# A hybrid decoder trunk on eight cores: two programs chosen by a per-core role instead of one program with a flag

## The chip, the cores and the metric

One Trainium2 chip, eight cores, one launch. Each of four sequences of 4096 tokens is shared by two cores: the even one has the first part, the odd one the second. The metric is device time in microseconds (us) of the slowest core. Some executions fall into a slower state, in which the cores of a die (cores 0 to 3, or 4 to 7) show a lower granted clock (TensorE's clock, as a share of full speed); they are kept apart, and only fast runs (or the cores of the undisturbed die) are compared. TensorE does the matmuls (PE in the profiles; PEld are its weight loads), VectorE (DVE), ScalarE (ACT) and GpSimd (POOL) the rest; SyncE (SP) and GpSimd issue the transfers (DMA).

## The reference, cut to what matters

```python
D_MODEL, BATCH, SEQ = 2048, 4, 4096
def reference(x, ...):
    h = x
    # layer 0: mLSTM, 8 heads, causal convolution of 4 taps on q and k, a state
    #   (C: 256x512, n: 256 per head) carried from the first token to the last
    h = h + mlstm_layer(rmsnorm(h, g0), ...)
    # layer 1: gMLP, spatial gating inside chunks of 128 tokens
    h = h + gmlp_layer(rmsnorm(h, g1), ...)
    return rmsnorm(h, gf)
```

Only the mLSTM state and three tokens of the convolution tie the second part of a sequence to the first. A chunk below is 128 tokens; a sequence has 32.

## The kernel before

Every core runs the same program. A *prefix* of 16 chunks gets the state at the split cheaply: per pair of heads the weighted keys K, then G = X^T K, then C = G^T W_v, without values, outputs or layer 1. Then 16 main chunks run through both layers in tiles of 6, 5, 5 chunks; each tile reads all weights (72 tiles of 2048x512, float32 in memory, cast to bfloat16 by the transfer) once. On even cores the prefix computes the wrong thing, and its outcome is multiplied by a flag of 0.

```python
MAIN = [6, 5, 5]
PRE = 16
...
        sizes = {16: [1, 1, 2, 3, 3, 3, 3], 17: [1, 2, 2, 3, 3, 3, 3]}[P]   # token groups of the k projection
...
        def nb_(c):                      # norm of prefix chunk c; its result is spilled to memory
            norm_b(px[c % 3][:], [pxb[c % 3]], pn[c % 2][:], pnb[c % 2], sl[c])
            xld(c + 3)
            dma("sp", xwsem[c % 2], xs_d[:, :, c * 256:(c + 1) * 256]..., pn[c % 2][:]..., R=[pnb[c % 2]], W=[xsd_b[c]])
        def run_stage(i):
            if i < P: na(i)              # square and sum on ScalarE
            if 0 <= i - 1 < P: nb_(i - 1)
            if 0 <= i - 2 < P: nc_(i - 2)    # transposes on TensorE, copies on ScalarE
            ...
        def xload():                     # the spilled activations come back, 1 MB at a time, 32 times, two buffers
            ...
            dma("sp", xrsem[i], XSt[:, i, 0:P, :]..., xs_d[j][:, 0:P * 256], R=xsd_b, W=[XSb[i]])
        def gpair(hp, jp, k):            # one group of G = X^T K: P matmuls of 512 columns
            ...
        def cgrp(hp, hh, cc, wi, q):
            ...
            dve([pkb, flagb], [cstgb[cc]], "tensor_scalar", out=cstg[:, cc, :], in0=pk[:, :], scalar1=flag[:, 0:1], ...)
...
    prefix(PRE, 0)
    for t in range(len(MAIN)):
        layer0(t, False)
        ...
```

The softmax here doesn't subtract the row's maximum and nothing guards it: scores larger than these inputs give would overflow.

Of the kernel before, what the change touches and what calls it, by code (L numbers as in the profile page):

```python
# [14 lines left out]
D = 2048  # L15
KC = 16
H = 8
EPS = 1e-6
NMAX = 6
PMAX = 16  # L20
MAIN = [6, 5, 5]
PRE = 16
NTOK = sum(MAIN) * 128
NPRE = PRE * 128
XP = 4 + NMAX * 128
XPP = 4 + PMAX * 128

# [180 lines left out]
def build_program():  # L208
    nc = bass.Bass("TRN2", target_bir_lowering=False)
    dt = lambda n, s, k="ExternalInput", d=F32: nc.dram_tensor(n, s, d, kind=k).ap()  # L210
    xm_d = dt("xm", [NTOK, D])
    xp_d = dt("xp", [NPRE, D])
    flag_d = dt("flag", [128, 1])
    wt_d = dt("wt", [NTILE, 128, KC * 512])
    wg_d = dt("wg", [128, KC * 16])
    g0_d = dt("g0bc", [128, D])
    g1_d = dt("g1bc", [128, D])
    gf_d = dt("gfbc", [128, D])
    convw_d = dt("convw", [128, 32 * 4])
    convb_d = dt("convb", [128, 32])  # L220
    gateb_d = dt("gateb", [128, 16])
    hg_d = dt("hgbc", [128, 4096])
    lng_d = dt("lng", [128, 32])
    lnb_d = dt("lnb", [128, 32])
    wsT_d = dt("wsT", [128, 8 * 128])
    bs_d = dt("bsbc", [128, 8 * 128])
    maskT_d = dt("maskT", [128, 128])
    ident_d = dt("ident", [128, 128])
    out_d = dt("out", [NTOK, D], "ExternalOutput")
    cst_d = nc.dram_tensor("cst", [H, 128, 1024], F32).ap()  # L230
    rs_d = nc.dram_tensor("rsd", [128, 1024], F32).ap()
    xs_d = nc.dram_tensor("xsd", [8, 128, PMAX * 256], BF16).ap()

    with ExitStack() as es:
        sems = {k: es.enter_context(nc.semaphore("s_" + k)) for k in ("pe", "act", "dve", "pool", "sp")}
        dsems = [es.enter_context(nc.semaphore("d%d" % i)) for i in range(100)]
        mem = Mem(nc)
        PSN = ["PJ0", "PJ1", "PJ2", "PT", "PS", "PN", "PK0", "PK1"]
        banks = [es.enter_context(nc.psum_tensor("ps_" + n, [128, 512], F32)) for n in PSN]
        body(nc, mem, TK(nc, sems, dsems), banks, locals())  # L240
    return nc


def body(nc, mem, tk, banks, dr):
    xm_d, xp_d, wt_d, out_d = dr["xm_d"], dr["xp_d"], dr["wt_d"], dr["out_d"]
# [19 lines left out]
    G = const("G", [D], F32); Gb = G.buf()  # L265
    flag = const("flag", [1], F32); flagb = flag.buf()
    convw = const("convw", [32, 4], F32); convwb = convw.buf()
# [42 lines left out]
    XO = HO + NMAX * 8192  # L310
    assert XO + 24576 <= REND, (XO + 24576, REND)

# [8 lines left out]
    def gtemps(tag, o_, n):  # L321
# [8 lines left out]
    GTM, _e = gtemps("m", _e, NMAX)  # L330
    (xnb0, xnb1), _e = seq(XO + 16384, [("xnb0", [D], BF16), ("xnb1", [D], BF16)])
    STG = [[(t, t.buf()) for t in (xs0,)], [(t, t.buf()) for t in (xnb0, xnb1)]]
    HN = NMAX // 2 * 128
    (acc, qT, kT, kp, so, sz), _e = seq(XO, [
# [19 lines left out]
    ybfb = [ybf.buf(i, i * 1024, i * 1024 + 1024) for i in range(2)]  # L354
    (uT, szT, sv, bia, junk1), _e = seq(XO, [
        ("uT", [4, NMAX * 128], BF16), ("szT", [3, HN], BF16), ("sv", [2, HN], F32),
        ("bia", [2, 128], F32), ("junk1", [512], BF16)])
    uTb = [[uT.buf((d_, i)) for i in range(2)] for d_ in range(4)]
# [122 lines left out]
    def consts():  # L481
        dma("pool", tk.dsem(), ident[:], dr["ident_d"], W=[identb])
        wpiece()
        wpiece()
        dma("pool", tk.dsem(), wg[:].rearrange("p k c -> p (k c)"), dr["wg_d"], W=[wgb])
        wpiece()
        wpiece()
        cload(convw[:], dr["convw_d"].rearrange("p (c j) -> p c j", j=4), convwb)
        cload(convb[:], dr["convb_d"], convbb)
        cload(gateb[:], dr["gateb_d"], gatebb)  # L490
        cload(maskT[:], dr["maskT_d"], maskTb)
        cload(flag[:], dr["flag_d"], flagb)
        cload(lng[:], dr["lng_d"], lngb)
        cload(lnb[:], dr["lnb_d"], lnbb)
        for b_ in cbufs:
            b_.w = (cs.sem, cs.cnt, cs.key)
        for t_, b_, v_ in ((onesf, onesfb, 1.0), (onesb, onesbb, 1.0), (mhalf, mhalfb, -0.5)):
            tk.op("dve", lambda v, t_=t_, v_=v_: v.memset(t_[:], v_), (), [b_])
# [82 lines left out]
    def prefix(P, tile0):  # L581
        NP = P * 128
        sizes = {16: [1, 1, 2, 3, 3, 3, 3], 17: [1, 2, 2, 3, 3, 3, 3]}[P]
        tgs = [(128 * sum(sizes[:i]), 128 * sum(sizes[:i + 1])) for i in range(len(sizes))]
# [22 lines left out]
        cstgb = [cstg.buf(i, i * 2048, i * 2048 + 2048) for i in range(2)]  # L607
        PGT, _e = gtemps("p", A4 + 7168, P)
        assert _e <= REND, (_e, REND)
        px = [mem.at("px%d" % i, [D], F32, a) for i, a in enumerate((A1, A1 + 8192, A2))]  # L610
# [131 lines left out]
        def nsum(hp):  # L742
            mm(KPb + [onesbb], [PSb], [(PS[:, hh * 2 + cc:hh * 2 + cc + 1], KP[:, c, hh * 256 + cc * 128:hh * 256 + (cc + 1) * 128],
                                        onesb[:, 0:1], c == 0, c == P - 1) for hh in range(2) for cc in range(2) for c in range(P)])
            dve([PSb, flagb], nstb[hp * 2:hp * 2 + 2], "tensor_scalar", out=nst[:, hp * 2:hp * 2 + 2, :],
                in0=PS[:, 0:4].rearrange("p (h c) -> p h c", c=2), scalar1=flag[:, 0:1], scalar2=None, op0=ALU.mult)

        def cgrp(hp, hh, cc, wi, q):
# [5 lines left out]
            if q == 0:  # L754
                return
            dve([pkb, flagb], [cstgb[cc]], "tensor_scalar", out=cstg[:, cc, :], in0=pk[:, :], scalar1=flag[:, 0:1], scalar2=None, op0=ALU.mult)
            dma("sp", css[cc], cst_d[h][:, cc * 512:(cc + 1) * 512], cstg[:, cc, :], R=[cstgb[cc]], W=[])
# [50 lines left out]
        def save_halo():  # L808
            dve([XTb[P - 1], flagb], [halob], "tensor_scalar", out=halo[:, :, 1:4], in0=XT[:, :, 4 + NP - 3:4 + NP],
                scalar1=flag[:, 0:1], scalar2=None, op0=ALU.mult)  # L810
        S.at(S.last, save_halo)
# [57 lines left out]

    def layer0(t, zero_state):  # L870
        n = MAIN[t]
# [141 lines left out]
        def head_events(h, oid, vid, zid):  # L1013
            b = vid[0]
            S.at(oid[1], lambda: ktr(h, list(range(h0))))
            S.at(oid[2], lambda: cb0(h))
            S.at(oid[3], lambda: ktr(h, list(range(h0, n))))
            if h + 1 < H:
# [15 lines left out]
        for h in range(H):  # L1034
            qk(h)
            oid = tm(T_O, h, ev_o)
            vid = tm(T_V, h, ev_v)
# [165 lines left out]

    prefix(PRE, 0)
    for t in range(len(MAIN)):
        layer0(t, False)
        n = MAIN[t]
# [35 lines left out]
def _prep_inputs(inputs):  # L1243
# [38 lines left out]
    for c in range(8):  # L1282
        b, s = c // 2, c % 2
        m = dict(common)
        m["xm"] = np.ascontiguousarray(x[b, s * NTOK:(s + 1) * NTOK])
        m["xp"] = np.ascontiguousarray(x[b, 0:NPRE])
        m["flag"] = np.full((128, 1), float(s), np.float32)
        in_maps.append(m)
# [14 lines left out]
```

## Time and profile before

| | us |
|---|---|
| median of the first three runs | 4950.75 |
| profiled run, slowest core (3) | 4951.6 |
| of this: prefix, up to the first main q/k projection | 676.6 |
| tile of 6 chunks, tile of 5, last tile of 5 | 1599.3, 1336.9, 1338.9 |

How to read it: the tiles have TensorE busy nearly without a gap, so a tile costs its columns; the prefix has 98 us in which TensorE waits. All eight cores have a prefix: it ends between 662.1 us (core 1) and 676.6 us (core 3), and from there on every core takes the same 4275.0 us. So cores with the same work differ by 14.5 us there. The lines themselves are in the prediction; in its table of stages the engines stand in the order PE, PEld, DVE, ACT, POOL, each with its busy us and (x instructions).

### The profile page before, as it was taken

How to read it: one execution, taken by the hardware profiler on the slowest of the kernel's cores; microseconds unless marked ns; L12 is line 12 of the kernel's file. 1: busy time of each engine (PE TensorE's matmuls, PEld its weight loads, DVE VectorE, ACT ScalarE, POOL GpSimd, SP SyncE). 2: the span in 40 equal slices, each digit the busy share in tenths (PEclk: the TensorE clock that was granted, in tenths of full speed). 3: DMA queues.
4: the chain of work that ended last, by engine and by line, in shares of the span. 5: the costliest groups of instructions: out<-in, count | busy, mean ns of one | idle time of the engine just before them, and what ended most of it. 6: DMA issues, size and time to landing. Idle time of an engine off the chain costs nothing.

```text
span 4951.6 us, 79527 instructions; the slowest of 8 cores (4937.1 to 4951.6 us)
## 1 busy us (share of the span) xinstructions
PE 4837.9 (98%) x29172; PEld 2630.9 (53%) x29172; DVE 1713.9 (35%) x3254; ACT 1707.8 (34%) x3242; POOL 677.6 (14%) x1314
## 2 busy tenths in 40 slices
PE   4999999999999999999999999999999999999999
PEld 3545545545544456645555544577455555445764
DVE  4614434434422033324453521133253444112331
ACT  4512334444422422213444413322144444143220
POOL 2100011111111110011111111111111111111111
PEclk8999999999999999999999999999999999999999
DMA  8555475655665565567666687776786667867765
GB/s 203 133 162 104 120 165 100 121 96 96 122 144 102 111 107 99 106 142 166 131 119 128 127 161 132 125 127 116 170 166 123 117 112 132 162 124 130 118 115 119
DMA packets 183196, 637.73 MB, mean 129 GB/s; under 512 B 19488, under 2 KB 36256, under 8 KB 171424
## 3 DMA queue, kind: packets, MB, share of 16 engines
q0 software_dynamic: 131616, 478.31, 55.4%
q1 hardware_dynamic: 51200, 154.35, 9.8%
q8 instruction: 240, 3.93, 0.3%
q14 instruction: 140, 1.15, 0.1%
HBM read 1072.55 MB, written 38.27 MB: 224 GB/s over the span
## 4 chain that ended last, share of the span: by engine, by line
PE 94%; DMA 3%; ACT 1%; DVE 1%; issue 1%; SPq 0%; DVEq 0%; ACTq 0%; POOL 0%; POOLq 0%
PE ps_PJ L159 80%; PE ps_PK L159 7%; PE ps_PN L159 5%; PE ps_PT L157 1%; DMA sb_xst<-xsd 1%; PE ps_PS L159 1%; DMA sb_px_120<-xp 1%; DMA xsd<-sb_pn_121 0%; DVE sb_pacc L146 0%; DMA xsd<-sb_pn_122 0%; ACT sb_xnT L143 0%; PE ps_PS L157 0%; DVE sb_H L146 0%; ACT L143 0%; SPq L168 0%
## 5 line engine op out<-in xcount | busy, mean ns | idle before, releaser
L159 PE MATMUL ps_PJ<-sb_w_72,sb_xnT 128*128 128x512 bf16 x2816 | 626.5, 379 | 0.0
L159 PE MATMUL ps_PJ<-sb_w_73,sb_xnT 128*128 128x512 bf16 x2816 | 625.3, 379 | 0.0
L159 PE MATMUL ps_PJ<-sb_w_71,sb_xnT 128*128 128x512 bf16 x2560 | 570.6, 379 | 0.0
L159 PE MATMUL ps_PJ<-sb_xnT,sb_w_71 128*128 128x384 bf16 (+3 forms) x3456 | 519.1, 309 | 1.7 <-DVE sb_acc L146 1.7
L159 PE MATMUL ps_PJ<-sb_xnT,sb_w_72 128*128 128x384 bf16 (+3 forms) x3072 | 463.7, 309 | 0.0
L159 PEld LDWEIGHTS ps_PJ<-sb_w_73,sb_xnT 128*128 128x128 bf16 x2816 | 273.2, 98 | 317.2
L159 PEld LDWEIGHTS ps_PJ<-sb_w_72,sb_xnT 128*128 128x128 bf16 x2816 | 272.7, 98 | 314.6
L159 PEld LDWEIGHTS ps_PJ<-sb_xnT,sb_w_71 128*128 128x128 bf16 x3456 | 334.2, 98 | 162.2 <-issue 2.2
L159 PE MATMUL ps_PJ<-sb_xnT,sb_w_73 128*128 128x384 bf16 (+3 forms) x2688 | 402.6, 309 | 0.0
L159 PEld LDWEIGHTS ps_PJ<-sb_w_71,sb_xnT 128*128 128x128 bf16 x2560 | 247.9, 98 | 286.9
L159 PEld LDWEIGHTS ps_PJ<-sb_xnT,sb_w_72 128*128 128x128 bf16 x3072 | 296.5, 98 | 141.1
L146 DVE SCALAR_TENSOR_TENSOR sb_acc<-ps_PJ,sb_convw,sb_acc 128x384 f32<-128x384 f32 (+1 forms) x576 | 323.9, 572 | 129.5 <-ACT sb_acc L143 88.7
L168 POOL DMA_DIRECT2D sb_w_72<-wt x304 | 163.2, 547 | 1205.4 <-PE ps_PJ L159 720.5
L159 PEld LDWEIGHTS ps_PJ<-sb_xnT,sb_w_73 128*128 128x128 bf16 x2688 | 260.1, 98 | 123.8
L168 POOL DMA_DIRECT2D sb_w_73<-wt x304 | 169.7, 569 | 892.6 <-PE ps_PJ L159 462.2
L143 ACT ACT_TABLE_LOAD x155 | 198.9, 1283 | 255.8 <-PE ps_PJ L159 190.5
L168 POOL DMA_DIRECT2D sb_w_71<-wt x304 | 164.1, 550 | 821.0 <-PE ps_PJ L159 451.0
L146 DVE SCALAR_TENSOR_TENSOR sb_STt<-ps_PS,sb_beta_57,sb_maskT 128x128 bf16<-128x128 f32 x128 | 44.9, 351 | 590.5 <-PE ps_PS L159 590.3
L159 PE MATMUL ps_PJ<-sb_kpp,sb_xst 128*128 128x512 bf16 x1024 | 230.6, 387 | 17.1 <-DMA sb_xst<-xsd 16.1
L146 DVE TENSOR_TENSOR sb_H<-ps_PJ,sb_H 128x512 f32<-128x512 f32 x72 | 49.8, 692 | 514.5 <-PE ps_PJ L159 514.4
L149 POOL TENSOR_SCALAR sb_sm<-sb_sm 128x1 f32<-128x1 f32 x192 | 50.7, 264 | 1265.2 <-ACT sb_junk_96 L143 638.4
L143 ACT ACTIVATE sb_Cb<-sb_C 128x512 bf16<-128x512 f32 (+1 forms) x232 | 156.2, 673 | 187.2 <-DVE sb_C L146 170.3
(237 smaller groups left out, 5701.6 us busy)
## 6 DMA issues: line engine op xcount, KB each, us to landing
sb_w_71<-wt POOLq DMA_DIRECT2D x304, 512.0 KB, 10.5
sb_w_72<-wt POOLq DMA_DIRECT2D x304, 512.0 KB, 10.4
sb_w_73<-wt POOLq DMA_DIRECT2D x304, 512.0 KB, 10.3
sb_xst<-xsd SPq DMA_DIRECT2D x32, 1024.0 KB, 5.0
sb_H<-xm SPq DMA_DIRECT2D x32, 512.0 KB, 20.9
out<-sb_H SPq DMA_DIRECT2D x16, 1024.0 KB, 7.5
sb_C<-cst SPq DMA_DIRECT2D x48, 256.0 KB, 17.8
sb_xs_77<-xm SPq DMA_DIRECT2D x10, 1024.0 KB, 7.6
```

The lines of the kernel that those rows point to most:

```text
L143: return self.op("act", lambda a: a.activation(**k), R, W)
L146: return self.op("dve", lambda v: getattr(v, m)(**k), R, W)
L149: return self.op("pool", lambda v: getattr(v, m)(**k), R, W)
L157: ins = p.transpose(out=o[0], in_=o[1], identity=o[2])
L159: ins = p.matmul(o[0], lhsT=o[1], rhs=o[2], start=o[3], stop=o[4])
L168: self.eng[e].dma_start(out=out, in_=in_).then_inc(ds.sem, 16)
```

## The change

The intent: even cores needn't run a prefix, so each core gets the program that it needs, and the time saved on even cores is shared by moving the split. Even cores (role 0) take 17 chunks in tiles of 6, 6, 5 with no prefix; odd cores (role 1) a prefix of 17 chunks and 15 chunks in tiles of 5, 5, 5. The role is a register loaded at the start; both programs stand in one instruction stream per engine behind a branch. The diff, cut to its core:

```diff
-MAIN = [6, 5, 5]
-PRE = 16
+ROLES = [(0, [6, 6, 5]), (17, [5, 5, 5])]
+NPRE = 17 * 128
...
-        body(nc, mem, TK(nc, sems, dsems), banks, locals())
+        dr = locals()
+        role = nc.values_load(role_d, min_val=0, max_val=1, ...)
+        with nc.If(role == 0):
+            body(nc, mem, TK(nc, sems, dsems), banks, dr, *ROLES[0])
+        mem.bufs.clear()
+        with nc.Else():
+            body(nc, mem, TK(nc, sems, dsems), banks, dr, *ROLES[1])
...
-            dve([pkb, flagb], [cstgb[cc]], "tensor_scalar", ..., scalar1=flag[:, 0:1], scalar2=None, op0=ALU.mult)
+            dve([pkb], [cstgb[cc]], "tensor_copy", out=cstg[:, cc, :], in_=pk[:, :])
...
+    def cold_norm(t):            # start of role 0: loads and norms its first 6 chunks
+        ...                      # stage(i): square of chunk i, norm of i-1, transposes of i-2
...
+            if stage is not None and h == 0:
+                ...              # head 0 of the first tile: o projection chunk by chunk beside the norm, then q/k
...
-    prefix(PRE, 0)
+    if PRE:
+        prefix(PRE, 0)
+    else:
+        stage0 = cold_norm(0)
```

More of the change, by code (lines that the diff above doesn't have):

```diff
@@ L18 @@
 EPS = 1e-6
-NMAX = 6
-PMAX = 16
-MAIN = [6, 5, 5]
-PRE = 16
-NTOK = sum(MAIN) * 128
-NPRE = PRE * 128
-XP = 4 + NMAX * 128
-XPP = 4 + PMAX * 128
+ROLES = [(0, [6, 6, 5]), (17, [5, 5, 5])]
+NPRE = 17 * 128
+NTOK = 17 * 128
+LEN = [128 * sum(r[1]) for r in ROLES]
+OFF = [0, LEN[0]]
 T_QK, T_O, T_V, T_Z, T_W0, T_V1, T_U1, T_Z1, T_W1, T_K = 0, 8, 16, 24, 32, 40, 48, 56, 64, 72
@@ L212, in build_program @@
     xp_d = dt("xp", [NPRE, D])
-    flag_d = dt("flag", [128, 1])
+    role_d = dt("role", [1, 1], d=I32)
     wt_d = dt("wt", [NTILE, 128, KC * 512])
@@ L231, in build_program @@
     rs_d = nc.dram_tensor("rsd", [128, 1024], F32).ap()
-    xs_d = nc.dram_tensor("xsd", [8, 128, PMAX * 256], BF16).ap()
+    xs_d = nc.dram_tensor("xsd", [8, 128, NPRE * 2], BF16).ap()
     with ExitStack() as es:
@@ L239, in build_program, with body @@
         banks = [es.enter_context(nc.psum_tensor("ps_" + n, [128, 512], F32)) for n in PSN]
-        body(nc, mem, TK(nc, sems, dsems), banks, locals())
-    return nc
-def body(nc, mem, tk, banks, dr):
+        dr = locals()
+        role = nc.values_load(role_d, min_val=0, max_val=1, skip_runtime_bounds_check_because="the host passes 0 or 1")
+        with nc.If(role == 0):
[3 more added lines that the diff above has]
+            body(nc, mem, TK(nc, sems, dsems), banks, dr, *ROLES[1])
+    return nc
+def body(nc, mem, tk, banks, dr, PRE, MAIN):
+    NMAX = max(MAIN)
+    PMAX = PRE
+    XP = 4 + NMAX * 128
+    XPP = 4 + PMAX * 128
     xm_d, xp_d, wt_d, out_d = dr["xm_d"], dr["xp_d"], dr["wt_d"], dr["out_d"]
@@ L265, in body @@
     G = const("G", [D], F32); Gb = G.buf()
-    flag = const("flag", [1], F32); flagb = flag.buf()
     convw = const("convw", [32, 4], F32); convwb = convw.buf()
@@ L310, in body @@
     XO = HO + NMAX * 8192
-    assert XO + 24576 <= REND, (XO + 24576, REND)
+    assert XO + 4096 * NMAX <= REND, (XO, REND)
     def seq(o_, items):
@@ L330, in body @@
     GTM, _e = gtemps("m", _e, NMAX)
-    (xnb0, xnb1), _e = seq(XO + 16384, [("xnb0", [D], BF16), ("xnb1", [D], BF16)])
+    assert _e <= XO + 4096 * NMAX - 8192
+    (xnb0, xnb1), _e = seq(XO + 4096 * NMAX - 8192, [("xnb0", [D], BF16), ("xnb1", [D], BF16)])
+    assert _e <= REND
     STG = [[(t, t.buf()) for t in (xs0,)], [(t, t.buf()) for t in (xnb0, xnb1)]]
-    HN = NMAX // 2 * 128
+    HN = (NMAX + 1) // 2 * 128
     (acc, qT, kT, kp, so, sz), _e = seq(XO, [
@@ L354, in body @@
     ybfb = [ybf.buf(i, i * 1024, i * 1024 + 1024) for i in range(2)]
-    (uT, szT, sv, bia, junk1), _e = seq(XO, [
-        ("uT", [4, NMAX * 128], BF16), ("szT", [3, HN], BF16), ("sv", [2, HN], F32),
-        ("bia", [2, 128], F32), ("junk1", [512], BF16)])
+    (junk1, uT, szT, sv, bia), _e = seq(XO, [
+        ("junk1", [512], BF16), ("uT", [4, NMAX * 128], BF16), ("szT", [3, HN], BF16), ("sv", [2, HN], F32),
+        ("bia", [2, 128], F32)])
     uTb = [[uT.buf((d_, i)) for i in range(2)] for d_ in range(4)]
@@ L491, in consts @@
         cload(maskT[:], dr["maskT_d"], maskTb)
-        cload(flag[:], dr["flag_d"], flagb)
         cload(lng[:], dr["lng_d"], lngb)
@@ L582, in prefix @@
         NP = P * 128
-        sizes = {16: [1, 1, 2, 3, 3, 3, 3], 17: [1, 2, 2, 3, 3, 3, 3]}[P]
+        sizes = [1, 2, 2, 3, 3, 3, 3]
         tgs = [(128 * sum(sizes[:i]), 128 * sum(sizes[:i + 1])) for i in range(len(sizes))]
@@ L607, in prefix @@
         cstgb = [cstg.buf(i, i * 2048, i * 2048 + 2048) for i in range(2)]
-        PGT, _e = gtemps("p", A4 + 7168, P)
-        assert _e <= REND, (_e, REND)
+        PGT, _e = gtemps("p", A4 + 3072, P)
+        assert A4 + 7168 <= REND, (A4, REND)
         px = [mem.at("px%d" % i, [D], F32, a) for i, a in enumerate((A1, A1 + 8192, A2))]
@@ L744, in nsum @@
                                         onesb[:, 0:1], c == 0, c == P - 1) for hh in range(2) for cc in range(2) for c in range(P)])
-            dve([PSb, flagb], nstb[hp * 2:hp * 2 + 2], "tensor_scalar", out=nst[:, hp * 2:hp * 2 + 2, :],
-                in0=PS[:, 0:4].rearrange("p (h c) -> p h c", c=2), scalar1=flag[:, 0:1], scalar2=None, op0=ALU.mult)
+            dve([PSb], nstb[hp * 2:hp * 2 + 2], "tensor_copy", out=nst[:, hp * 2:hp * 2 + 2, :],
+                in_=PS[:, 0:4].rearrange("p (h c) -> p h c", c=2))
         def cgrp(hp, hh, cc, wi, q):
@@ L755, in cgrp @@
                 return
-            dve([pkb, flagb], [cstgb[cc]], "tensor_scalar", out=cstg[:, cc, :], in0=pk[:, :], scalar1=flag[:, 0:1], scalar2=None, op0=ALU.mult)
+            dve([pkb], [cstgb[cc]], "tensor_copy", out=cstg[:, cc, :], in_=pk[:, :])
             dma("sp", css[cc], cst_d[h][:, cc * 512:(cc + 1) * 512], cstg[:, cc, :], R=[cstgb[cc]], W=[])
@@ L808, in save_halo @@
         def save_halo():
-            dve([XTb[P - 1], flagb], [halob], "tensor_scalar", out=halo[:, :, 1:4], in0=XT[:, :, 4 + NP - 3:4 + NP],
-                scalar1=flag[:, 0:1], scalar2=None, op0=ALU.mult)
+            dve([XTb[P - 1]], [halob], "tensor_copy", out=halo[:, :, 1:4], in_=XT[:, :, 4 + NP - 3:4 + NP])
         S.at(S.last, save_halo)
@@ L868, in norm_tile, with ld, stage, start @@
         return ie + 1
-    def layer0(t, zero_state):
+    def cold_norm(t):
+        n = MAIN[t]
+        cx = [mem.at("cx%d" % i, [D], F32, YO + i * 8192) for i in range(3)]
+        cxb = [t_.buf() for t_ in cx]
+        cn = [mem.at("cn%d" % i, [D], BF16, YO + 24576 + i * 4096) for i in range(2)]
+        cnb = [t_.buf() for t_ in cn]
+        cj = mem.at("cj", [D], BF16, YO + 32768)
+        cjb = cj.buf()
+        csem = [tk.dsem() for _ in range(3)]
+        sl = {}
+        def ld(c):
+            if c < n:
+                dma("sp", csem[c % 3], cx[c % 3][:], xm_d[c * 128:(c + 1) * 128, :], W=[cxb[c % 3]])
+        def stage(i):
+            if i < n:
+                sl[i] = rsq_slots()
+                norm_a(cx[i % 3][:], [cxb[i % 3]], cj[:], cjb, sl[i])
+            if 0 <= i - 1 < n:
+                c = i - 1
+                norm_b(cx[c % 3][:], [cxb[c % 3]], cn[c % 2][:], cnb[c % 2], sl[c])
+                ld(c + 3)
+            if 0 <= i - 2 < n:
+                c = i - 2
+                norm_c(cn[c % 2][:], cnb[c % 2], XNT, 4 + c * 128, XNTb[c], [(PT, PTb), (PN, PNb)], ("act", "act"))
+            if 0 <= i - 3 < n:
+                gates_mm(n, i - 3)
+        def start():
+            ld(0)
+            load_G(dr["g0_d"])
+            ld(1)
+            consts()
+            ld(2)
+            tk.op("dve", lambda v: v.memset(XNT[:, :, 0:4], 0.0), (), [XNTh])
+        S.add(start)
+        S.rate[-1] = 0.0
+        return stage
+    def layer0(t, zero_state, stage=None):
         n = MAIN[t]
@@ L1014, in head_events @@
             b = vid[0]
-            S.at(oid[1], lambda: ktr(h, list(range(h0))))
+            first = stage is not None and h == 0
+            S.at(vid[0] if first else oid[1], lambda: ktr(h, list(range(h0))))
             S.at(oid[2], lambda: cb0(h))
-            S.at(oid[3], lambda: ktr(h, list(range(h0, n))))
+            S.at(vid[2] if first else oid[3], lambda: ktr(h, list(range(h0, n))))
             if h + 1 < H:
@@ L1034, in layer0 @@
         for h in range(H):
-            qk(h)
-            oid = tm(T_O, h, ev_o)
+            if stage is not None and h == 0:
+                wi0 = len(tiles)
+                for i in range(3):
+                    S.add(lambda i=i: stage(i))
+                    S.rate[-1] = 0.0
+                oid = tm(T_O, h, ev_o)
+                for i in range(n):
+                    S.at(oid[i], lambda i=i: stage(i + 3))
+                S.at(S.last + 2, lambda: gates_lf(n, GTM))
+                S.at(S.last + 3, lambda: gates_main(n, GTM))
+                S.at(S.last + 8, wsetup0)
+                S.at(S.last + 20, wsetup1)
+                S.at(S.last + 22, wsetup2)
+                qk(h)
+            else:
+                qk(h)
+                oid = tm(T_O, h, ev_o)
             vid = tm(T_V, h, ev_v)
@@ L1202, in post_fin @@
         return post
-    prefix(PRE, 0)
+    stage0 = None
+    if PRE:
+        prefix(PRE, 0)
+    else:
+        stage0 = cold_norm(0)
     for t in range(len(MAIN)):
-        layer0(t, False)
+        layer0(t, not PRE and t == 0, stage0 if t == 0 else None)
         n = MAIN[t]
@@ L1284, in _prep_inputs @@
         m = dict(common)
-        m["xm"] = np.ascontiguousarray(x[b, s * NTOK:(s + 1) * NTOK])
-        m["xp"] = np.ascontiguousarray(x[b, 0:NPRE])
-        m["flag"] = np.full((128, 1), float(s), np.float32)
+        m["xm"] = np.zeros((NTOK, D), np.float32)
+        m["xm"][:LEN[s]] = x[b, OFF[s]:OFF[s] + LEN[s]]
+        m["xp"] = x[b, 0:NPRE]
+        m["role"] = np.full((1, 1), s, np.int32)
         in_maps.append(m)
@@ L1300 @@
         b, s = c // 2, c % 2
-        out[b, s * NTOK:(s + 1) * NTOK] = res.results[c]["out"]
+        out[b, OFF[s]:OFF[s] + LEN[s]] = res.results[c]["out"][:LEN[s]]
     return out
```

## The prediction

> **What bounds the kernel now.** I read the page of the slowest core first (busy times, then the chain), then the waits of TensorE, then a table of stages, then the matmuls kept apart by shape. The page of the kernel before:
>
> ```profile
> PE 4837.9 (98%) x29172; PEld 2630.9 (53%) x29172; DVE 1713.9 (35%) x3254; ACT 1707.8 (34%) x3242; POOL 677.6 (14%) x1314
> ...
> PE 94%; DMA 3%; ACT 1%; DVE 1%; issue 1%; SPq 0%; DVEq 0%; ACTq 0%; POOL 0%; POOLq 0%
> ```
>
> TensorE is busy for all but 113.7 us of 4951.6, and the chain that ended last lies on it for 94%. So the time is the sum of TensorE's work plus about 110 us of waits. Where these waits lie shows in the table of stages. I cut it where TensorE's timeline goes over to another stage: at 676.6 the first q/k projection of tile 0 (6 chunks) follows the prefix, at 2275.85 that of tile 1 (5 chunks), at 3612.7 that of tile 2 (5 chunks). Columns: stretch, its length, then the busy time of each engine, clock, DMA share, GB/s.
>
> ```profile
> 0.00:120.00 120.00, 52.91 (x678) 46.13 (x679) 49.10 (x87) 56.20 (x86) 23.46 (x38) 0.89 0.89 209
> 120.00:228.00 108.00, 98.24 (x798) 61.89 (x797) 78.09 (x123) 71.82 (x111) 15.78 (x19) 0.97 0.51 125
> ...
> 676.60:2275.85 1599.25, 1598.83 (x8997) 824.99 (x8996) 532.41 (x989) 534.62 (x1025) 212.14 (x419) 1.00 0.60 114
> 2275.85:3612.70 1336.85, 1335.53 (x8037) 738.35 (x8036) 458.65 (x900) 471.66 (x909) 205.24 (x403) 1.00 0.73 137
> 3612.70:4951.60 1338.90, 1325.22 (x7841) 729.30 (x7839) 436.25 (x860) 456.36 (x889) 196.39 (x388) 1.00 0.68 128
> ```
>
> The reader is to see three things. The tiles are bound by TensorE without a gap: 0.4 us idle in the tile of six chunks, 1.3 us in the middle tile of five, and 13.7 us in the last one, nearly all of it the end (last norm and store). The first 120 us are bound by transfers (DMA busy 89%, TensorE busy 44%). And every core, also those whose sequence starts at zero, runs the prefix of 676.6 us and multiplies its outcome by a flag of 0 or 1. The longest waits of TensorE, all of them in the prefix:
>
> ```profile
> PE ps_PT L157 <- DVE sb_pn_121 L146: 27.1, 3, 15.9
> PE ps_PJ L159 <- ACT sb_pxT L143: 21.6, 1, 21.6
> PE ps_PJ L159 <- DVE sb_pacc L146: 20.8, 8, 9.7
> PE ps_PJ L159 <- DMA sb_xst<-xsd: 16.1, 4, 6.0
> ```
>
> **What the Trainium skill says.** (1) "Perfetto Trace Analysis", Identifying the Most-Contended Engine: busy share of matmuls is no good measure of the distance to the roofline. Here it doesn't mislead: counting the columns of all matmuls in the instruction list gives 11.29 million, at 2.4 GHz 4704 us, 95% of the span; little but fewer columns helps. (2) "TensorE: Matmul & The Clock Gate", Back-to-back issue gap: an isolated gap of N/2.4 + 2.5 ns, 216 ns for 512 columns and 109 for 256, but about 131 ns for 512 in a stream with weight loads. The trace agrees with the first within some per cent (222.5 and 119.4 ns below) and not with the 131. (3) "Runtime: NRT & Kernel Launch", Instruction fetch mechanics and the preamble's breakdown: fetching is sequential, a taken branch to a far target waits for its page; a register load from HBM is about 1.3 us. (4) "Advanced Engine Details and Errata", Control Flow Timing: compare-and-branch about 108 ns. The trace before has neither branch nor register load in its work, so it shows nothing on (3) and (4).
>
> **The change part by part.** There are now two programs, and the time is the slower one. Even cores (role 0): 17 chunks in tiles of 6, 6, 5 without a prefix. Odd cores (role 1): prefix of 17 chunks, then tiles of 5, 5, 5. Against the kernel before, the odd core has one main chunk less and one prefix chunk more.
>
> *Odd cores, main part.* Three tiles of five take 1336.85 + 1336.85 + 1338.90 = 4012.6 us, where 1599.25 + 1336.85 + 1338.90 = 4275.0 stood: minus 262.4 us. This is a measured difference of tiles, so it already holds the worse form of a tile of five, whose feature-major products split 384 + 256 columns instead of 384 + 384.
>
> *Odd cores, prefix.* From the groups of matmuls by shape:
>
> ```profile
> L159 PE MATMUL ps_PJ<-sb_w_72,sb_xnT 128*128 128x512 bf16 x2816 | 626.5, 379 | 0.0
> L159 PE MATMUL ps_PJ<-sb_kpp,sb_xst 128*128 128x512 bf16 x1024 | 230.6, 387 | 17.1 <-DMA sb_xst<-xsd 16.1 <-DVE sb_GT L146 0.9
> L159 PE MATMUL ps_PJ<-sb_xnT,sb_w_72 128*128 128x256 bf16 x640 | 76.4, 273 | 0.0
> L159 PE MATMUL ps_PJ<-sb_xnT,sb_w_71 128*128 128x259 bf16 x384 | 46.8, 275 | 0.0
> L159 PE MATMUL ps_PJ<-sb_pxT,sb_w_72 128*128 128x131 bf16 x384 | 24.7, 222 | 3.7 <-DVE sb_pacc L146 3.4
> ```
>
> Busy time over count is the cost in the stream (the mean duration overlaps its neighbours): 626.5/2816 = 222.5 ns for 512 columns, 121.9 for 259, 64.3 for 131, 225.2 for the prefix's X-times-K product. The k projection's token groups go from 1,1,2,3,3,3,3 to 1,2,2,3,3,3,3 chunks: 4 head pairs x 4 blocks x 16 = 256 matmuls widen from 131 to 259 columns, 256 x 57.6 ns = 14.7 us. The product gains one matmul in each of 64 groups: 64 x 225.2 ns = 14.4 us. Transposes of the chunk and its keys (32 at about 0.08 us), gates and key sums: about 3.6 us. Tile 0's norm inside the prefix has 5 chunks instead of 6: minus 1.9 us. The spilled activations reloaded (32 loads, 16.1 us of waits) grow by a sixteenth: plus 1.0 us. In the opening one chunk more must be read (1 MB) and spilled (0.5 MB), at 209 GB/s 7.5 us, of which about 9 us of the above work counted for that stretch can take part: I put down 3 us on top. Sum: 14.7 + 14.4 + 3.6 - 1.9 + 1.0 + 3 = 34.8 us, a prefix of 711.
>
> *Start.* On each engine two register loads and a compare-and-branch now stand before the first load: 2 x 1.3 + 0.1 us, and the odd cores jump over the other program, some 1 to 2 us for the page. I take 4 us, an estimate from the pages named, once, all engines side by side.
>
> *The flag.* Multiplications by the flag become copies of equal shape: 40 instructions off the bound engine, nothing.
>
> *Odd cores' sum:* 676.6 + 34.8 + 4 + 4012.6 = 4728.0 us in the span; the median reported before is 0.85 us under the profiled span, so 4727.
>
> *Even cores.* 1599.25 + 1599.25 + 1338.90 = 4537.4 us for the tiles. In the kernel before the first product starts at 39.3 us, held by chunk loads and by transposes' copies waiting in ScalarE's order behind the third chunk's load; the same order stands in the new start. The first head's o projection then takes chunks as they land, estimated at 10 us each as late in the old opening, instead of 3.6: with six chunks about 39 + 50 - 18 = 71 us over the tile's own work, plus about 8 us of its own norm and gates, minus some 4 us for the state products that fall away at zero state. About 4612 us. So odd cores set the end with some 115 us to spare; this imbalance costs but can't be moved by whole chunks: one chunk back would add 262 - 33 there.
>
> **The rivals.** (a) *Even cores become the bound.* It needs a cold start of over 190 us. For: TensorE stood still 67 us of the first 120. Against: no spill (xsd) competes there, weights come from the queue at the same pace. If so: 4730 to 4780. (b) *The tiles of five starve for weights.* A tile reads the same weights for fewer products; DMA share rises from 0.60 to 0.73. Against: both tiles of five run with no weight wait already, all eight cores at once. If the first did starve: 10 to 40 us more. (c) *Two programs cost fetches.* If jumps or longer code made engines wait at each page, tens of us. Against: straight code streams now (5 MB on the instruction queues, 0.4% of DMA time), and only one jump is taken before the work and one after. I allow 10 us. (d) *The opening takes the whole cost of a chunk twice:* DMA is 89% busy there, and the changed groups need five instead of four norm stages before the second job; a prefix of 725 instead of 711, time 4742. (e) *It gains more:* with the even cores out of the prefix their transfers no longer meet in the opening, 10 to 15 us less there: 4713.
>
> **Range and chances.** The main term (262) is the difference of two measured tiles, good to about 3 us. The prefix has plus or minus 12, the start minus 2 to plus 10. So 4706 to 4752, with 4727 in it. Within 2% means above 4852, which would take 125 us of a cost that I don't see: 4% with rival (a) at its worst or a start I have misread. Faster by over 2%: 0.95, slower 0.01.
>
> **What would show it.** In the changed profile the slowest core is an odd one, its span about 4727, with its first main q/k projection at about 715 (711 and the branch), main tiles of 1337 each, TensorE idle at most 2 us in the first two. Even cores end near 4612, first o product near 40 us. TensorE's clock stays at 0.99. I am wrong if an even core is the slowest, if the first projection on odd cores starts after 735, if their tiles take over 1345 us, or if engines wait at the start beyond 10 us.

## The result, and the profile after

Four runs gave 4694.42, 4694.98, 4749.18 and 5533.51 us; two more, both fast, 4694.36 and 4696.15. The last two of the four are slow ones: their die 1 had a mean clock of 0.98 and 0.83, while die 0 in the same runs ended at 4693. So the median of the four, 4722.08, says little; the fast runs stand at 4694 to 4696. The ratio of the fast runs to the fast runs of before is 0.9471 (interval 0.944 to 0.9502). Ratios here are the mean time of one kernel's fast runs over that of the other's of the same rounds, so not quite the ratio of the medians that are quoted. Faster by over 2%, as said, but by 33 us more than said: the fast runs lie 11 us under the low end of the range.

The page of the kernel after, of core 1; it and core 3, also an odd one, are the slowest with 4693.1 us each, and everything after the page is of core 3:

```profile
PE 4597.1 (98%) x28308; PEld 2562.5 (55%) x28308; DVE 1640.4 (35%) x3163; ACT 1650.1 (35%) x3133; POOL 675.3 (14%) x1294
...
PE 95%; DMA 2%; ACT 1%; DVE 1%; issue 1%; SPq 0%; POOL 0%; DVEq 0%; ACTq 0%; POOLq 0%
```

It is bound as before. The table of stages (stretch, length, busy time of the engines, clock, DMA share, GB/s), cut at the prefix's end and between the tiles:

```profile
0.00:683.10 683.10, 602.42 (x4396) 355.92 (x4397) 292.18 (x505) 252.54 (x428) 68.18 (x106) 0.98 0.56 150
683.10:2018.76 1335.66, 1335.24 (x8037) 738.56 (x8036) 453.39 (x898) 469.70 (x907) 203.93 (x399) 1.00 0.71 136
2018.76:3356.23 1337.47, 1335.58 (x8037) 738.26 (x8036) 458.50 (x901) 471.63 (x909) 205.60 (x403) 1.00 0.71 137
3356.23:4693.10 1336.87, 1324.85 (x7841) 729.42 (x7839) 436.00 (x860) 456.44 (x889) 198.04 (x388) 1.00 0.67 128
```

The reader is to see that the three tiles take 4010.0 us where 4012.6 were predicted, and the prefix with the start 683.1 where 676.6 + 34.8 + 4 = 715.4 were. All of the miss but 2.6 us is in the first line: 17 chunks took 6.5 us more than 16 had taken. TensorE's busy time there grew by 24.1 us (578.3 to 602.4); its idle time *fell* by 17.6 us (98.3 to 80.7), although the later start now stands in it. The waits of TensorE in the kernel after:

```profile
PE ps_PT L154 <- DVE sb_pn_44378 L143: 25.1, 2, 24.2
PE ps_PJ L156 <- ACT sb_pxT L140: 19.3, 1, 19.3
PE ps_PJ L156 <- DVE sb_pacc L143: 19.0, 8, 6.7
PE ps_PJ L156 <- DMA sb_xst<-xsd: 4.7, 3, 3.6
```

The wait for reloaded activations (the last line) is 4.7 us instead of 16.1. The start shows in the queue of SyncE. Core 3, which jumps to its program, then core 0, which falls through (start us, duration, what):

```profile
6.45 4.62 SPq L165 DMA_DIRECT2D sb_px_44375<-xp  x1
11.13 0.42 SPq L165 DMA_DIRECT2D sb_G<-g0bc  x1
```

```profile
2.52 0.39 SPq L165 DMA_DIRECT2D sb_cx_122<-xm  x1
2.96 0.42 SPq L165 DMA_DIRECT2D sb_G<-g0bc  x1
```

Before, the first load was issued at 1.06 us. The second load, behind the long first issue, comes 8.2 us later on core 3 than on core 0. Even cores end at 4609 to 4610 us, 84 us before the odd ones.

### The profile page after: what moved, and what is told of

Same layout as the page of the kernel before. It is cut to its first block, busy times and chain, and to the rows that moved or that the text cites. A ratio compares the mean times of both kernels' runs of the same rounds, so it can differ in the third digit from the quotient of the medians.

```text
span 4693.1 us, 77314 instructions; the slowest of 8 cores (4609.1 to 4693.1 us)
## 1 busy us (share of the span) xinstructions
PE 4597.1 (98%) x28308; PEld 2562.5 (55%) x28308; DVE 1640.4 (35%) x3163; ACT 1650.1 (35%) x3133; POOL 675.3 (14%) x1294
## 4 chain that ended last, share of the span: by engine, by line
PE 95%; DMA 2%; ACT 1%; DVE 1%; issue 1%; SPq 0%; POOL 0%; DVEq 0%; ACTq 0%; POOLq 0%
PE ps_PJ L156 81%; PE ps_PK L156 6%; PE ps_PN L156 5%; PE ps_PT L154 1%; PE ps_PS L156 1%; DMA sb_px_44377<-xp 1%; DMA xsd<-sb_pn_44379 1%; DVE sb_pacc L143 1%; DMA sb_xst<-xsd 0%; ACT sb_xnb_44340 L140 0%; DVE sb_H L143 0%; PE ps_PN L154 0%; SPq L165 0%; ACT L140 0%; ACT sb_xnT L140 0%
## 5 line engine op out<-in xcount | busy, mean ns | idle before, releaser
L156 PE MATMUL ps_PJ<-sb_w_44329,sb_xnT 128*128 128x512 bf16 x2640 | 587.8, 379 | 0.0
L156 PE MATMUL ps_PJ<-sb_w_44330,sb_xnT 128*128 128x512 bf16 x2640 | 586.7, 379 | 0.0
L156 PE MATMUL ps_PJ<-sb_w_44328,sb_xnT 128*128 128x512 bf16 x2400 | 535.2, 379 | 0.0
L156 PE MATMUL ps_PJ<-sb_xnT,sb_w_44328 128*128 128x384 bf16 (+3 forms) x3456 | 487.9, 300 | 1.7 <-DVE sb_acc L143 1.7
L156 PE MATMUL ps_PJ<-sb_xnT,sb_w_44329 128*128 128x256 bf16 (+3 forms) x3072 | 435.9, 300 | 0.0
L156 PEld LDWEIGHTS ps_PJ<-sb_w_44330,sb_xnT 128*128 128x128 bf16 x2640 | 256.0, 98 | 296.9
L156 PEld LDWEIGHTS ps_PJ<-sb_w_44329,sb_xnT 128*128 128x128 bf16 x2640 | 255.5, 98 | 294.0
L156 PEld LDWEIGHTS ps_PJ<-sb_w_44328,sb_xnT 128*128 128x128 bf16 x2400 | 232.5, 98 | 268.4
L156 PE MATMUL ps_PJ<-sb_xnT,sb_w_44330 128*128 128x256 bf16 (+3 forms) x2688 | 378.4, 300 | 0.0
L143 DVE SCALAR_TENSOR_TENSOR sb_acc<-ps_PJ,sb_convw,sb_acc 128x384 f32<-128x384 f32 (+1 forms) x576 | 308.1, 549 | 119.4 <-ACT sb_acc L140 77.2
L143 DVE SCALAR_TENSOR_TENSOR sb_pacc<-ps_PJ,sb_convw,sb_pacc 128x384 f32<-128x384 f32 (+2 forms) x336 | 179.2, 540 | 89.8 <-ACT sb_pacc L140 60.9
## 6 DMA issues: line engine op xcount, KB each, us to landing
sb_C<-cst SPq DMA_DIRECT2D x48, 256.0 KB, 15.5
```

The lines of the kernel that those rows point to most:

```text
L143: return self.op("dve", lambda v: getattr(v, m)(**k), R, W)
L156: ins = p.matmul(o[0], lhsT=o[1], rhs=o[2], start=o[3], stop=o[4])
```

## The experiments

Two theories for the missing 32 us in the prefix. **C, contention:** the transfers of the odd cores' prefix were slowed by the even cores running one too; with those gone, the waits fall. **P, pattern:** 17 chunks hide their own transfers better than 16 did (a group of G has 17 matmuls instead of 16 to cover a reload; the second token group is wider), whatever the neighbours do.

**e1_all_odd_no_branch: the odd cores' program on all eight cores, no branch.**

```diff
-        with nc.If(role == 0):
-            body(..., *ROLES[0])
-        mem.bufs.clear()
-        with nc.Else():
-            body(..., *ROLES[1])
+        body(..., *ROLES[1])
```

> All eight cores run the odd cores' program (17-chunk prefix, tiles 5, 5, 5) with no branch; even cores' outputs are wrong on purpose. Changed kernel, odd core 3: first main projection at 683.1 us, of which some 5.4 us are the start; 80.7 us of TensorE idle before it, reload waits 4.7 us. Theory C (the waits fell because even cores no longer run a prefix beside the odd ones): with all eight in the prefix the waits come back, first projection of the slowest core at 697 to 706, reload waits 12 to 18 us, span 4707 to 4716. Rival P (the 17-chunk prefix hides its transfers better by itself, whatever the neighbours do): 677 to 679, reload waits about 5, span about 4688.

Three fast runs, 4706.0 to 4710.7; profiled spans 4696.1 to 4705.0. The first main projection came at 694.0 us on the slowest cores (685.2 to 694.0), reload waits 11.2 to 15.6 us. That lies between the theories: the reload waits are back, as C says, but the prefix is 3 us shorter than C's lowest. P has a small share: in the mean of the eight cores the reload waits are 13.1 us, not the 16.9 of before. A 17th chunk, with all cores alike, costs 694.0 - 676.6 = 17.4 us by these two profiles. They are one execution each, and before's span of 4951.6 us lies above the 4946.9 to 4949.5 of the other fast runs here. Taken over fast runs of one chip, the longest span less the profiled time of the tiles (4275.0 and 4011.1 us) leaves 673.0 us for before (six runs; a seventh, with die 0 at 0.987 to 0.991, left out) and 696.4 for e1 (three runs): 23.4 us. So the chunk costs 17 to 23 us, half to two thirds of the 34.8 predicted.

**e2_all_odd_branch: the changed kernel with role 1 passed to all cores.**

```diff
-        m["role"] = np.full((1, 1), s, np.int32)
+        m["role"] = np.full((1, 1), 1, np.int32)
```

> The changed kernel with role 1 passed to all eight cores, so the branch and its register loads stay and all cores jump; even cores' outputs wrong on purpose. Against e1 it shows the start's cost alone: 5.4 us in the first load's issue, 4 to 8 us in the span. Theory C: span 4712 to 4722, first projection at 702 to 712. Rival P: span 4692 to 4696, first projection at 683.

Of four runs two were slow, and in the profiled one die 1 had a clock of 0.989 to 0.993, so I read die 0: first projection at 696.7 to 701.1 us, spans 4706.8 to 4711.2. Against e1's die 0 (686.6 to 694.0) the start costs 7.1 us on the slowest, 7.5 in the mean. Both numbers are a us short of the low ends that C gave, and 15 to 18 us above P's. Over the undisturbed die of all four runs, reckoned as for e1, the start costs 5.3 us. Same instructions, same jump, other neighbours: the changed kernel's odd cores are 18.0 us earlier (683.1; over all fast runs 17.9). Core 3 of e2, split at the first product with reloaded activations:

```profile
0.00:235.60 235.60, 162.77 (x1512) 116.83 (x1513) 133.45 (x212) 133.99 (x202) 43.47 (x59) 0.95 0.70 171
235.60:701.10 465.50, 446.60 (x2888) 241.32 (x2886) 158.83 (x293) 118.35 (x227) 23.80 (x47) 0.98 0.54 133
```

**e3_odd_alone: meant to leave the even cores idle; it didn't.**

```diff
-        with nc.If(role == 0):
-            body(..., *ROLES[0])
-        mem.bufs.clear()
-        with nc.Else():
+        with nc.If(role == 1):
             body(..., *ROLES[1])
```

> Even cores skip everything (outputs missing on purpose), odd cores run their program alone. Theory C: even fewer transfers beside it, first main projection at 665 to 680 on odd cores, span 4675 to 4690. Rival P: as in the changed kernel, 683 and 4693. If the even cores' work slows the tiles too, they would fall below 1336 us each; I expect no change there (within 1 us).

The compiled program held the register loads but no branch, and all eight cores ran the odd program (spans 4697.9 to 4710.0). So its expectation wasn't tested. It serves as a control: e1 plus register loads. The first load was issued at 2.3 to 2.6 us instead of 1.06, and the first projection came at 694.8 us in the mean of the cores against 690.8 in e1. The loads alone are some 1.4 us at the queue; their 4 us at the prefix's end are within the spread of cores (687 to 700).

**e4_no_rebalance: the change's first part alone.** Even cores skip the prefix; the split stays at 16 chunks.

```diff
-ROLES = [(0, [6, 6, 5]), (17, [5, 5, 5])]
-NPRE = 17 * 128
+ROLES = [(0, [6, 5, 5]), (16, [6, 5, 5])]
+NPRE = 16 * 128
...
-        sizes = [1, 2, 2, 3, 3, 3, 3]
+        sizes = [1, 1, 2, 3, 3, 3, 3]
```

> The change's first part alone: branch on the role, even cores run 16 chunks (6, 5, 5) without prefix, odd cores the old 16-chunk prefix and 16 chunks (6, 5, 5); result correct. The work on odd cores is that of the kernel before. Theory C: the old 16-chunk prefix gets faster too, first projection at 650 to 662 instead of 662 to 677 although the start costs 5 us, span 4925 to 4937. Rival P: first projection at 670 to 682, span 4950 to 4957.

Fast runs 4932.03 and 4932.21 (two of four were slow), correct. The old 16-chunk prefix on odd cores now ends at 654.1 to 656.9 us instead of 662.1 to 676.6, with the start in it. This is what C said and P did not allow: the odd cores' work is the old one but for the flag's multiplications and the addresses of some buffers. The next four fences split the prefix at the first product with reloaded activations, first the kernel before (core 3), then e4 (core 5):

```profile
0.00:228.30 228.30, 151.45 (x1477) 108.22 (x1478) 127.38 (x210) 128.31 (x196) 39.35 (x58) 0.93 0.71 169
228.30:676.62 448.32, 426.86 (x2825) 230.07 (x2825) 159.21 (x296) 116.82 (x224) 24.49 (x49) 0.97 0.55 136
```

```profile
0.00:222.50 222.50, 150.14 (x1476) 107.61 (x1477) 127.02 (x210) 128.16 (x196) 40.73 (x58) 0.95 0.67 173
222.50:656.86 434.36, 424.70 (x2826) 229.67 (x2825) 158.14 (x296) 116.89 (x224) 24.53 (x49) 0.99 0.52 142
```

The same with 17 chunks: e1 (core 3, neighbours in a prefix too), then the kernel after (core 3, neighbours without):

```profile
0.00:228.60 228.60, 159.67 (x1512) 114.77 (x1513) 133.18 (x212) 134.14 (x202) 41.65 (x59) 0.95 0.71 176
228.60:693.93 465.33, 447.19 (x2888) 241.54 (x2886) 158.96 (x293) 118.45 (x227) 23.79 (x47) 0.98 0.54 134
```

```profile
0.00:233.30 233.30, 160.27 (x1512) 115.84 (x1513) 133.39 (x212) 134.19 (x202) 44.38 (x59) 0.95 0.67 174
233.30:683.11 449.81, 442.16 (x2889) 240.07 (x2886) 158.79 (x293) 118.36 (x227) 23.81 (x47) 0.99 0.50 138
```

Two things are to be seen. In the second part, neighbours without a prefix are worth 14.0 us (448.3 to 434.4) with 16 chunks and 15.5 (465.3 to 449.8) with 17 (14.1 and 12.5 in the means of the cores that run a prefix); of the 14.0, 11.8 are TensorE's waits (21.5 to 9.7) and the rest its busy time, whose clock rises from 0.97 to 0.99. In the first part (the opening) the 17th chunk adds 8.2 us of busy time from before to e1, and the length stays (228.3 and 228.6): its work went into waits that were there anyway. In the mean of the eight cores the opening grows by 3.9 us (224.8 to 228.7), so about half of the work is hidden rather than all of it.

**e7_roles_by_pair: whose neighbour?** Four prefixes as in the changed kernel, but two to a pair of cores.

```diff
-        m["role"] = np.full((1, 1), s, np.int32)
+        m["role"] = np.full((1, 1), 1 - b % 2, np.int32)
```

> The changed kernel with the roles dealt otherwise: cores 0, 1, 4, 5 run the prefix program, cores 2, 3, 6, 7 the one without; outputs wrong on purpose. As in the changed kernel four cores run a prefix, but each beside a neighbour (0 with 1, 4 with 5) that runs one too. If the contention is between such neighbours: first main projection of cores 0, 1, 4, 5 at 697 to 702, as with all eight (e2), reload waits 12 to 18 us. If it is shared by the whole chip or a die: about 683, reload waits 4 to 6 us, as in the changed kernel.

Both runs fast. First projection on cores 0, 1, 4, 5 at 692.6, 702.0, 697.8 and 699.2 us, reload waits 12.3 to 14.2 us: as in e2, not as in the changed kernel (core 0 is 4 us below what was expected). So it is the neighbour in the pair that counts, not the number of prefixes on the chip or die. Spans of e7, die 0:

```profile
core 0: 4702.6 us, clock 0.995
core 1: 4712.0 us, clock 0.994
core 2: 4611.1 us, clock 0.998
core 3: 4610.0 us, clock 0.998
```

The Trainium skill, "Trainium Kernel Development and Optimization", NeuronCore Architecture, says that main memory is 24 GiB per pair of cores. That pairs, and not dies, hinder each other agrees with a memory that a pair shares; the traces don't show at which point the transfers meet.

**e8_odd_alone: even cores idle, this time in fact.**

```diff
+        small = es.enter_context(...)        # 128 x 8
         with nc.If(role == 0):
-            body(..., *ROLES[0])
-        mem.bufs.clear()
+            nc.vector.memset(small[:], 0.0)
         with nc.Else():
             body(..., *ROLES[1])
```

> e3 as it was meant: even cores do one small memset and end, odd cores run their program with no work beside it (outputs wrong on purpose). Contention: first projection earlier than the changed kernel's 683, at 670 to 681, since the even cores' own loads fall away; tiles unchanged at 4010. Rival (neighbours without influence): 683 and 4693.

Cores 1, 3 and 5 have their first projection at 654.1 to 655.9 us, 27 to 29 us before the changed kernel, more than I expected; tiles 4010.6 to 4010.8 as expected. Not all of this is the neighbours' doing: the odd cores stand in the second arm here too, but behind a first arm of one memset, and they issue their first load at 2.5 us, not at 6. Against e9 below, whose odd cores also begin at 2.5 us (666.0 and 667.0), it is 10 to 13 us. Core 7 differs in both runs: 685.1 in the profiled one, with reload waits of 17.9 us although core 6 ended after 7.1 us. Cores 1 and 7, after the opening:

```profile
208.60:654.13 445.53, 440.89 (x2889) 240.08 (x2887) 158.88 (x293) 118.37 (x227) 23.80 (x47) 1.00 0.48 139
```

```profile
216.40:685.11 468.71, 447.97 (x2888) 241.47 (x2886) 158.73 (x293) 118.25 (x227) 23.80 (x47) 0.97 0.47 132
```

Three cores support C: the fewer transfers beside them, the fewer waits (reload waits 1.4 to 1.5 us). What held core 7 back I don't know; no run settles it.

**e9_arms_swapped: odd cores fall through, even cores jump.**

```diff
-        with nc.If(role == 0):
-            body(..., *ROLES[0])
+        with nc.If(role == 1):
+            body(..., *ROLES[1])
         mem.bufs.clear()
         with nc.Else():
-            body(..., *ROLES[1])
+            body(..., *ROLES[0])
```

> The changed kernel with the two arms swapped, so that odd cores fall through and even cores jump; correct. In the traces the first load of a core that falls through is issued at 2.5 us, of one that jumps at 5.2 to 6.7. If the jump is what e2 shows over e3, odd cores end 3 to 5 us earlier: 4688 to 4690. If it is hidden behind the opening's transfers: 4692 to 4694.

Fast runs 4682.46 and 4683.66, correct (four of six were slow; the profile fell in one, with die 1 undisturbed). The gain is 11 to 12 us, not 3 to 5. It all lies in the opening. Core 5:

```profile
0.00:216.70 216.70, 159.29 (x1513) 115.94 (x1514) 133.25 (x212) 134.13 (x202) 41.71 (x59) 0.96 0.71 186
216.70:665.96 449.26, 441.88 (x2887) 240.42 (x2885) 158.84 (x293) 118.11 (x227) 23.80 (x47) 0.99 0.50 138
```

216.7 us against 233.3, and then the same 449. A jump accounts for some 4 us of first issue, and the first issue itself is shorter (0.38 us instead of 3.8 to 5.0); together they bring the second load 8 us forward, half of the 16.6. The odd cores' spans fall by 15 us (means over fast runs 4692.9 and 4677.7), the device time by 12: it stands 1.0 to 1.4 us above the longest span in every run whose slowest core takes the second arm or has no branch, and 3.5 to 3.9 us in e9, e10, e12 and e14, where it takes the first. A jump over the other arm at the very end would explain this; no run tests it. The rest of the opening's gain asked for a cause: I supposed that of two neighbours the one whose loads are queued first gets on (theory N), against the jump and slow issue alone (rival J).

**e10_swapped_copy_first: e9 with ScalarE's order in the opening changed.**

```diff
-            if i < P: na(i)
-            if 0 <= i - 1 < P: nb_(i - 1)
             if 0 <= i - 2 < P: nc_(i - 2)
+            if i < P: na(i)
+            if 0 <= i - 1 < P: nb_(i - 1)
```

> e9, and in each stage of the prefix's norm the copy of chunk i-2 comes ahead of the square of chunk i on ScalarE, so that it no longer stands behind the third chunk's load (19 us of TensorE's wait in the changed kernel); correct. First product at about 27 us instead of 45. If the opening is bound by its order of work: 5 to 15 us less than e9, 4675 to 4684. If it is bound by transfers: the wait moves to the next chunk and the time stays within 3 us of e9.

Fast runs 4681.00 and 4681.92, correct; odd cores' spans 4674.1 to 4677.3 against e9's 4676.6 and 4677.7. The first product comes at 18.8 us (core 5) instead of 35.3, and then TensorE stands for 12.8 us at the next chunk. The wait moved, as the second expectation says. That speaks for an opening bound by its transfers; it excludes only this one change of the order of work.

**e11 to e14, on one more chip.** On it die 1 ran at 0.987 to 0.994 in the fast runs, so the whole-chip times are some 30 us up and I compare the odd cores 1 and 3 of die 0.

> The changed kernel unaltered, on the chip of the three below: fast runs at 4693 to 4697, opening (to the first product with reloaded activations) 233 us on odd cores.

The changed kernel again (no edit): cores 1 and 3 at 4692.1 and 4695.6 us, opening 231.7 and 235.6.

> e9 unaltered on the same chip. e9 ended 11 us before the changed kernel, all in the opening (217 against 233 us), more than the jump of 4 us explains. Here again: 4681 to 4685.

e9 again (no edit): 4682.6 and 4678.7 us, opening 220.0 and 221.1; over the fast runs of the chip the ratio to before is 0.9453 (0.943 to 0.9476) against 0.9494 (0.9475 to 0.9513) for e11.

The edit of e13 (and, with 20 in place of 5, of e14 on top of e9):

```diff
...
+            for i in range(5):
+                if i: nc.vector.wait_ge(late, i)
+                nc.vector.memset(idle[:], 0.0).then_inc(late, 1)     # 128 x 2048
+            nc.sync.wait_ge(late, 5)
+            nc.gpsimd.wait_ge(late, 5)
             body(..., *ROLES[0])
```

> The changed kernel, odd cores still jump, but even cores begin only after five memsets of 128x2048 in a chain, some 6 to 12 us later, so that they come after the odd ones. Correct. Theory N (in the opening it counts which of two neighbours sends its loads first): the odd cores' opening falls to 219 to 228 us although they jump as before, span 4679 to 4689. Rival J (the gain of the swap is the jump and the slow first load issue behind it alone): opening 233, span 4693 to 4696.

Even cores issued their first load at 14.3 us (core 0), odd ones at 5.6 and 5.8 after their jump. The odd openings fell to 224.5 and 225.4 us and the spans to 4681.0 and 4682.9. N's numbers held, J's didn't: nothing but the neighbours' start was changed. Core 1 of e11, then of e13, split as above:

```profile
0.00:231.70 231.70, 159.92 (x1512) 115.92 (x1513) 133.28 (x212) 133.95 (x202) 43.86 (x59) 0.96 0.67 175
231.70:682.15 450.45, 442.61 (x2888) 240.35 (x2886) 158.88 (x293) 118.45 (x227) 23.80 (x47) 0.99 0.51 137
```

```profile
0.00:224.50 224.50, 157.01 (x1512) 112.72 (x1513) 133.28 (x212) 134.03 (x202) 39.85 (x59) 0.97 0.70 180
224.50:670.78 446.28, 440.71 (x2888) 240.06 (x2885) 158.89 (x293) 118.50 (x227) 23.86 (x47) 1.00 0.51 139
```

Of the 11 us on core 1, 7 are won in the opening and 4 after it. Over all fast runs the mean span of cores 1 and 3 is 4692.7 us in e11, 4683.2 in e13 and 4678.8 in e12. So of the 13.9 us that the swap wins on this chip, 9.5 come with the order of the two neighbours alone; the other 4.4, by subtraction, are left for the jump. The long first issue depends on the neighbour too: after a jump it lasts 2.2 to 2.9 us where the neighbour jumps as well or begins later (e2, e7, e13), and 3.5 to 5.0 where the neighbour is already loading (after, e4, e9 to e12).

> e9, and even cores begin after twenty such memsets, some 25 to 45 us late, out of their slack of about 65 us. Correct. Theory N: odd cores' opening near that of a core with an idle neighbour (208.6 us in e8): 209 to 213, span 4668 to 4675, even cores at 4635 to 4665. Rival J: as e9, opening 217, span 4677 to 4684.

Even cores began at 53 us. Odd openings 220.9 and 220.1 us, spans 4682.6 and 4681.9: as e12, no nearer to the 208.6 of a core whose neighbour does nothing. Here N's numbers failed and the span fits J's. The trace shows why delaying more gains nothing. Up to 53 us TensorE on core 1 has been busy for 21.3 us, like core 1 of e8, whose neighbour is idle (21.5), and ahead of core 1 of e12 (15.5). From 53 to 120 us, with the even core's loads running, it is busy for 46.7 us, against 59.3 in e8 and 55.7 in e12. So the even core's loads cost the odd one time wherever they come within the opening; a head start of 3 to 9 us (e12, e13) helps, one of 50 us helps no more.

## Why the prediction was wrong, point by point

**Right:** the direction; odd cores as the bound; the main part, minus 262.4 said and minus 265.0 measured (4275.0 to 4010.0); even cores at 4612 said, 4609.1 to 4609.6 measured, their first o product near 40 said, 35.6 on core 0, and the five steps between the six chunks of its first head 44.2 us (35.6 to 79.8) where 50 were said, so the terms hold within 3 to 6 us, which in the sum cancel in part; the clock, 0.996. Rival (a), even cores as bound, and rival (b), starving tiles of five, are out: the even cores end 84 us early, and the first tile of five has 0.4 us of idle time. Rival (c), dear instruction fetch, came true only as the start.

**Wrong: the prefix with its start, 715.4 said, 683.1 measured.** Sum on the slowest undisturbed core, each term from a pair of profiles, and beside it from the longest spans of all fast runs, reckoned as for e1:

| term | said | profiles | all fast runs | from |
|---|---|---|---|---|
| 17th chunk | +34.8 | +17.4 | +23.4 | before to e1 (676.6 to 694.0) |
| start | +4 | +7.1 | +5.3 | e1 to e2, die 0 (694.0 to 701.1) |
| neighbours without a prefix | 0 | -18.0 | -17.9 | e2 to after (701.1 to 683.1) |
| sum | +38.8 | +6.5 | +10.8 | |

The failing step is the treatment of waits: "The spilled activations reloaded (32 loads, 16.1 us of waits) grow by a sixteenth: plus 1.0 us", and in the opening "I put down 3 us on top". I took the waits of the profile before as a property of the odd cores' program and added the chunk's work to them. First, and this is the larger part, they were in part the neighbour's doing: its prefix was to be removed by the very change, which is worth 18 us where I put 0 in the sum, and the reload waits went from 16.1 to 4.7 us. The trace before held a hint: eight cores with the same work ended their prefixes between 662.1 and 676.6 us. Second, work and waits didn't add up in the opening: TensorE's work for the chunk was close to what I said (30.8 us said; 8.2 in the opening and 20.3 after it measured, before to e1), but the opening grew by 0.3 us on core 3 and by 3.9 in the mean of the cores.

The path before, e4, after gives the same end: minus 19.7 for skipping the prefix on even cores with the start paid, plus 26.2 for the chunk (656.9 to 683.1); over all fast runs minus 16.0 and plus 26.8. That the chunk costs more beside quiet neighbours (26.2 us) than beside loud ones (17.4), since both effects fill the same waits, is likely but not shown: over all fast runs it is 26.8 against 23.4, and the longest spans of e1's three runs alone differ by 4.6 us.

Rival (e), "their transfers no longer meet in the opening, 10 to 15 us less there: 4713", named the cause, but not the place of the larger part, and so too small a size: from before to e4, 14.0 us are won after the opening, and 5.8 us in it in spite of the start. Rival (d), the opening paying twice, is out. The start cost 5 to 7 us against 4 said; the 1 to 2 us for the jump stood on no page and in no trace, and the 1.3 us for each register load took for one load what the page gives for a few words or registers together (see the last section). The jump shows as a later first issue and, what I hadn't thought of, it let the even cores' loads go first; e13 shows that this order is worth some 10 us.

**A version better than both** is e9 (arms swapped), 4682.5 and 4683.7 us against 4694 to 4696; e10's further 2 us are within what two runs can tell. The some 60 us of slack on its even cores can't be used by whole chunks: an extra main chunk there costs 262 us.

## What to carry to other kernels

A wait seen in a profile of one core may be made by another core's transfers; when a change takes work off that neighbour, the waits of the core that sets the time have to be estimated anew, and work added in a stage full of waits can cost less than its own time (here 8.2 us of work made the opening 0.3 to 3.9 us longer). Measure such a term from two runs that differ in the neighbour's work only. Where two programs share a branch, try letting the core that sets the end fall through and issue its first loads before its neighbour: here that was worth 12 us.

## What the Trainium skill lacked or had wrong

- "Runtime: NRT & Kernel Launch", Instruction fetch mechanics: it says that a taken branch to a far target stalls, but gives no size. Here the first load is issued at about 2.5 us on a core that falls through and at 5.1 to 6.7 us on one that jumps over the other program, and the first issue after the jump lasts 2.2 to 5.0 us instead of 0.38, longest where the neighbour is already loading. Over an arm of one memset (e8) nothing of this shows: 2.5 us and 0.38.
- The same page gives about 1.3 us for the preamble's stage of register loads, by its own words several registers' worth, and about 200 ns per register. Two loads on each engine moved the first issue by 1.3 to 1.5 us in all (from 1.06 to between 2.3 and 2.6 us, e3). That is near the figure of the whole stage and three times 2 x 0.2; my 2 x 1.3 counted the stage twice.
- "TensorE: Matmul & The Clock Gate", Back-to-back issue gap: about 131 ns per matmul of 512 columns in a stream with weight loads. Here it is 222.5 ns; the page's isolated gap, 216 ns, is near.
- What the ordinary transfers of a pair's two cores cost each other below their share of bandwidth I found on no page. "HBM Reference", Specifications (TRN2), says that they share a domain's bandwidth, about 358 GB/s for each when both stream, and asks for benchmarks with the pair active. Here the mean over the prefix is about 150 GB/s moved per core, with slices up to 375 in the opening (memory sees more, since weights are cast on the way: over the whole span 1074 MB are read where 638 are moved); the neighbour's prefix still costs 18 us of some 700, and the order in which two neighbours begin some 10 us.
